# Both feed-forward products of a transformer block as seven block products each

## The chip, the cores and the metric

The kernel runs on one core of a Trainium2 chip, in one launch. The metric is the device time of a run in microseconds; the kernel before and the changed one are compared by their medians. Five engines matter here: TensorE (PE in the views; PEld is its weight load, which overlaps), VectorE (DVE), ScalarE (ACT), GpSimd (POOL) and SyncE (SP), which only issues transfers here. Each works through its own instructions in order and waits on semaphores for the others.

## The reference, cut to what matters

A block of 512 tokens with 1024 features goes through a mixing layer (attention, spatial gating, a short convolution and a pooling branch, gated and merged) and then through a feed-forward layer. Everything is float32. The change concerns the last three lines.

```python
D_MODEL = 1024; SEQ = 512; D_FF = 4 * D_MODEL; EPS = 1e-6
...
        x = x + rmsnorm(merged @ w_out[l], norm_mix_post[l])
        h = rmsnorm(x, norm_ffn_pre[l])
        f = jnp.square(jax.nn.relu(h @ w_ff1[l])) @ w_ff2[l]
        x = x + rmsnorm(f, norm_ffn_post[l])
```

## The kernel before

Matrix products keep float32 accuracy with operands in the faster format fp32r: each operand is split into a high part (a cast, on ACT) and a low part (source minus high part, on DVE), and one product of blocks is three matmuls, high by high, high by low and low by high, added up in PSUM. That is `mm3`. `load` fetches 128x1024 weights into a ring of three `raw` buffers through SP's queue, and `split_w` makes the pair `wh`, `wl` out of them, in rings of five. PE and ACT run through the wrapper `InOrder`, so all their instructions carry line 95 (in the feed-forward layer it fixes the order of PE alone); `split_w`'s subtraction is line 119.

The normalized input of the feed-forward layer is kept transposed, as `hh` and `hl` (128 partitions x 8 blocks of features x 512 tokens). `turn_h(t)` makes the part of 128 tokens: eight transposes of `yg`, the cast, the subtraction, and the sum of squares for the norm. It is called for tokens t - 1 while the output projection of the mixing layer runs for tokens t, and for the last 128 tokens in the midst of the first feed-forward blocks.

The first product has 32 blocks of 128 hidden features. Four of them (`EARLY`) start with the first 256 tokens alone, since the last 128 tokens are not ready, and get their second half afterwards; these are the only matmuls of 256 columns in this layer. Each other block is 8 x 3 matmuls of 512 columns (`ff1`). A block's result goes through relu and square on ACT into `u`, and is split by `usplit`. The second product runs in two halves of 512 output features. The first half is interleaved: after each block of the first product come 4 x 3 matmuls of 512 columns for the block ahead of it (`second`). The second half follows by itself, 32 blocks long (L805 on); its last six blocks (`LAST`) are held back, and done for 128 tokens after the other, so that norm and store of one part run beside the matmuls of the next.

SP's queue holds the transfers in program order. Each waits until the buffer that it fills is free. On ACT, DVE and POOL a scheduler sets the order by its own estimate of times; PE keeps the order of the code.

Of the kernel before, what the change touches and what calls it, by code (L numbers as in the profile page):

```python
# [80 lines left out]
def build(ctx, tc, d, out):  # L81
# [102 lines left out]
    cs = zp.tile([P, 2, NT, 16], F32, name="cs")  # L184

# [473 lines left out]
    gmix = xp.tile([P, D], F32, name="gmix")  # L659
    gffn = xp.tile([P, D], F32, name="gffn")  # L660
# [37 lines left out]
    def turn_h(t):  # L698
        for j in range(2):
# [5 lines left out]
            DVE.tensor_tensor(dst[1], pt, f(hh_)[:, 4 * j:4 * j + 4, t * P:(t + 1) * P], ALU.subtract)  # L705
        sq = wk_.tile([P, D], F32, tag="sq", name="sq", bufs=2)
# [43 lines left out]
    acc = [bank("acc") for _ in range(NT)]  # L750

    pend = []

    def usplit(j):
        uj = u[j // 8][:, j % 8, :]
        uh = us.tile([P, S], F32R, tag="uh", name="uh")
        ul = us.tile([P, S], F32R, tag="ul", name="ul")
        DVE.tensor_copy(uh, uj)
        DVE.tensor_tensor(ul, uj, f(uh), ALU.subtract)  # L759
        return uh, ul  # L760

    def ff2(dst, j, w, us_, t, first=0, last=NFF - 1):
        mm3(dst[t], sl(us_, slice(None), slice(t * P, (t + 1) * P)), sl(w, slice(None), slice((j % 2) * 512, (j % 2 + 1) * 512)),
            j == first, j == last)
# [24 lines left out]
    while pend:
        second(*pend.pop(0))  # L790
    for t in range(NT):
        sq = us.tile([P, S], F32, tag="r", name="r", bufs=2)
        ACT.activation(sq, acc[t], AF.Square, scale=r2[:, t:t + 1], accum_out=sst[:, t, 0:1])
        DVE.tensor_scalar(sst[:, t, 0:1], sst[:, t, 0:1], D * EPS, None, ALU.add)
        DVE.scalar_tensor_tensor(fo[:, t, :], acc[t], r2[:, t:t + 1], gpost[:, :512], ALU.mult, ALU.mult)
# [21 lines left out]
    for t in range(NT):
        for j, w, us_ in held:
            ff2(acc2, j, w, us_, t)
        sq = us.tile([P, S], F32, tag="r", name="r", bufs=2)  # L820
        f2 = lp.tile([P, D], F32, tag="f2", name="f2", bufs=2)
        ACT.activation(sq, acc2[t], AF.Square, scale=r2[:, t:t + 1], accum_out=sst[:, t, 1:2])
        norm_scale(sst[:, t, 2:3], sst[:, t, 3:4], sst[:, t, 0:1], sst[:, t, 1:2])
        DVE.scalar_tensor_tensor(f2[:, 512:], acc2[t], r2[:, t:t + 1], gpost[:, 512:], ALU.mult, ALU.mult)
        DVE.scalar_tensor_tensor(f2[:, :512], fo[:, t, :], sst[:, t, 2:3], x1[:, t, :512], ALU.mult, ALU.add)
        nc.sync.dma_start(out[t * P:(t + 1) * P, :512], f2[:, :512])
        DVE.scalar_tensor_tensor(f2[:, 512:], f2[:, 512:], sst[:, t, 2:3], x1[:, t, 512:], ALU.mult, ALU.add)
        nc.sync.dma_start(out[t * P:(t + 1) * P, 512:], f2[:, 512:])


def layout(i):
# [42 lines left out]
    g["w2"] = pairs(a["w_ff2"])  # L874
# [32 lines left out]
```

## Time and profile before

| | |
|---|---|
| median of 3 runs | 751.49 us (751.43 to 751.66) |
| the profiled execution | 751.82 us, of which the span from the first to the last instruction is 750.1 us |
| busy share of the span | PE 99%, PEld 84%, DVE 53%, ACT 37%, POOL 2% |
| mean granted clock of TensorE | 0.999 of full speed |
| DMA | 78.69 MB, 105 GB/s over the span |

A busy share is a mean over stages. A matmul's duration in the rows is longer than the distance to the next one's start, since matmuls are pipelined; the step from start to start is what one costs in a row of many. [...]

### The profile page before, as it was taken

How to read it: one execution, taken by the hardware profiler on the slowest of the kernel's cores; microseconds unless marked ns; L12 is line 12 of the kernel's file. 1: busy time of each engine (PE TensorE's matmuls, PEld its weight loads, DVE VectorE, ACT ScalarE, POOL GpSimd, SP SyncE). 2: the span in 40 equal slices, each digit the busy share in tenths (PEclk: the TensorE clock that was granted, in tenths of full speed). 3: DMA queues.
4: the chain of work that ended last, by engine and by line, in shares of the span. 5: the costliest groups of instructions: out<-in, count | busy, mean ns of one | idle time of the engine just before them, and what ended most of it. 6: DMA issues, size and time to landing. Idle time of an engine off the chain costs nothing.

```text
span 750.1 us, 8971 instructions
## 1 busy us (share of the span) xinstructions
PE 741.9 (99%) x3554; PEld 626.4 (84%) x3554; DVE 400.6 (53%) x673; ACT 276.3 (37%) x423; POOL 13.2 (2%) x28
## 2 busy tenths in 40 slices
PE   9999999999999999999999999999999999999996
PEld 8988888888888888888889888888888888888885
DVE  7599975366365456445376533343343343596624
ACT  6875543532332323232354422432332333321201
POOL 1110000000000000000000000000000000000001
PEclk9999999999999999999999999999999999999999
DMA  8433231272323232322304332233222223323103
GB/s 309 181 99 113 85 113 57 83 254 85 112 85 112 85 110 88 100 97 85 96 16 149 133 113 84 85 108 105 96 92 104 85 85 112 102 94 108 61 0 113
DMA packets 23146, 78.69 MB, mean 105 GB/s; under 512 B 3008, under 2 KB 3520, under 8 KB 23104
## 3 DMA queue, kind: packets, MB, share of 16 engines
q1 hardware_dynamic: 23072, 78.12, 31.2%
q8 instruction: 28, 0.46, 0.2%
q14 instruction: 14, 0.11, 0.0%
q0 software_dynamic: 32, 0.00, 0.0%
HBM read 76.01 MB, written 2.10 MB: 104 GB/s over the span
## 4 chain that ended last, share of the span: by engine, by line
PE 87%; DVE 7%; DMA 3%; ACT 2%; issue 1%; POOL 0%; SPq 0%; DVEq 0%; ACTq 0%; POOLq 0%
PE fb L95 26%; PE z L95 23%; PE acc L95 23%; PE wo L95 6%; PE y L95 6%; DMA xk<-in_x 2%; DVE wl L119 1%; DMA xT<-in_xT 1%; PE po L95 1%; DVE ql L537 1%; DVE kl L537 1%; PE s L95 0%; PE tr L95 0%; DVE m L596 0%; ACT sq L95 0%
## 5 line engine op out<-in xcount | busy, mean ns | idle before, releaser
L95 ACT CAST wh<-raw 128x1024 fp32r<-128x1024 f32 (+1 forms) x126 | 131.8, 1048 | 365.3 <-PE z L95 148.4
L119 DVE TENSOR_TENSOR wl<-raw,wh 128x1024 fp32r<-128x1024 f32 (+1 forms) x126 | 153.1, 1217 | 158.3 <-ACT wh L95 156.7
L95 PE MATMUL fb<-zh,wh 128*128 128x512 f32 x336 | 131.4, 391 | 0.1
L95 PE MATMUL fb<-zl,wh 128*128 128x512 f32 x336 | 130.9, 390 | 0.0
L95 PE MATMUL fb<-zh,wl 128*128 128x512 f32 x336 | 130.8, 389 | 0.0
L95 PE MATMUL z<-hh,wh 128*128 128x512 f32 (+1 forms) x288 | 105.4, 366 | 0.0
L95 PE MATMUL z<-hl,wh 128*128 128x512 f32 (+1 forms) x288 | 105.3, 365 | 0.0
L95 PE MATMUL z<-hh,wl 128*128 128x512 f32 (+1 forms) x288 | 105.2, 365 | 0.0
L95 PE MATMUL acc<-wh,uh 128*128 128x512 f32 x232 | 90.2, 389 | 0.0
L95 PE MATMUL acc<-wl,uh 128*128 128x512 f32 x232 | 90.2, 389 | 0.0
L95 PE MATMUL acc<-wh,ul 128*128 128x512 f32 x232 | 90.2, 389 | 0.0
L95 PEld LDWEIGHTS fb<-zh,wh 128*128 128x128 f32 x336 | 63.1, 188 | 13.3 <-DVE zc L349 0.4
L95 PEld LDWEIGHTS fb<-zh,wl 128*128 128x128 f32 x336 | 63.1, 188 | 13.2
L440 DVE TENSOR_TENSOR g<-fb,rbc 128x512 f32<-128x512 f32 x32 | 22.1, 692 | 96.8 <-PE fb L95 96.8
L95 PEld LDWEIGHTS fb<-zl,wh 128*128 128x128 f32 x336 | 63.1, 188 | 12.8
L95 PEld LDWEIGHTS z<-hh,wl 128*128 128x128 f32 x288 | 54.3, 189 | 8.8
L95 PEld LDWEIGHTS z<-hl,wh 128*128 128x128 f32 x288 | 54.3, 189 | 8.8
L95 PEld LDWEIGHTS z<-hh,wh 128*128 128x128 f32 x288 | 54.3, 189 | 8.6
L95 PEld LDWEIGHTS acc<-wl,uh 128*128 128x128 f32 x232 | 43.5, 188 | 9.1
L95 PEld LDWEIGHTS acc<-wh,uh 128*128 128x128 f32 x232 | 43.5, 188 | 9.0
L95 PEld LDWEIGHTS acc<-wh,ul 128*128 128x128 f32 x232 | 43.5, 188 | 9.0
L759 DVE TENSOR_TENSOR ul<-u,uh 128x512 fp32r<-128x512 f32 x58 | 40.1, 692 | 3.2
(253 smaller groups left out, 851.1 us busy)
## 6 DMA issues: line engine op xcount, KB each, us to landing
raw<-in_w SPq DMA_DIRECT2D x64, 512.0 KB, 3.3
raw<-in_wG SPq DMA_DIRECT2D x32, 512.0 KB, 3.4
raw<-in_wF SPq DMA_DIRECT2D x10, 512.0 KB, 3.8
raw<-in_wB SPq DMA_DIRECT2D x8, 512.0 KB, 3.3
raw<-in_wO SPq DMA_DIRECT2D x8, 512.0 KB, 3.3
xk<-in_x SPq DMA_DIRECT2D x4, 512.0 KB, 10.0
x<-in_x SPq DMA_DIRECT2D x4, 512.0 KB, 5.1
out<-f SPq DMA_DIRECT2D x8, 256.0 KB, 2.0
```

Of the source, the lines that this page charges most:

```text
L95: ins = op(*a, **k)
L119: DVE.tensor_tensor(lo[:, :n], raw[:, :n], f(hi)[:, :n], ALU.subtract)
L440: DVE.tensor_tensor(g, ps, rbc, ALU.mult)
L537: DVE.tensor_tensor(dst[1][rows, :], src, f(dst[0])[rows, :], ALU.subtract)
L759: DVE.tensor_tensor(ul, uj, f(uh), ALU.subtract)
```

## The change

Strassen's scheme (Winograd's form) multiplies 2 x 2 blocks with seven block products in place of eight, and with sums and differences of blocks ahead of them and behind.

In the first product the two halves are those of the 512 tokens (256 each), of the 1024 input features (4 blocks of 128 each), and two neighbouring blocks of 128 hidden features. Three sums of input blocks (`hsum`) are made in `turn_h` and a fourth after the early blocks (`s4`, put where `hh`'s block A21 was). The early four blocks stay as they are. Each of 14 pairs of weight blocks loads `left` and `rght`, makes four differences of 128x512 on POOL (`sub`), splits 128x1024 three times and 128x512 once, and does seven parts of 4 x 3 matmuls of 256 columns. Partial sums that are needed twice are copied out of PSUM (`small`) and added on DVE.

The second product no longer runs beside the first. It runs in three passes over 16 pairs of hidden blocks: two block products in the first, three in the second, two in the third, each product 2 x 3 matmuls of 512 columns for each pair. Weight blocks are stored as four quarters (`quads`). The differences of activations are made in place on POOL, those of weights on POOL and, one of three in the second pass, on DVE. Six pairs' quarter b21 is kept (`KEPT`); all else is loaded anew for each pass. Norm, residual and store come at the end, with the last two pairs (`LAST`) held back.

```diff
@@ turn_h @@
+        if t >= NT // 2:
+            r = slice((t - NT // 2) * P, (t - NT // 2 + 1) * P)
+            v = wk_.tile([P, 3, HK, P], F32, tag="sv", name="sv", bufs=2)
+            v1, v2, v3 = (v[:, c] for c in range(3))
+            DVE.tensor_tensor(v3, f(hh_)[:, :HK, r], pts[0], ALU.subtract)
+            POOL.tensor_tensor(v3, v3, f(hl_)[:, :HK, r], ALU.add)
+            DVE.tensor_copy(v1, pts[0])
+            DVE.tensor_tensor(v1, v1, pts[1], ALU.add)
+            DVE.tensor_tensor(v2, pts[1], v3, ALU.subtract)
+            for c in (slice(0, 1), slice(1, 3)):
+                ACT.copy(hsum[0][:, c, :, r], v[:, c])
+                DVE.tensor_tensor(hsum[1][:, c, :, r], v[:, c], f(hsum[0])[:, c, :, r], ALU.subtract)
@@ first product @@
+    POOL.tensor_tensor(s4, f(hh_)[:, HK:, :HS], f(hsum[0])[:, 1], ALU.subtract)
+    POOL.tensor_tensor(s4, s4, f(hl_)[:, HK:, :HS], ALU.add)
+    POOL.tensor_tensor(s4, s4, f(hsum[1])[:, 1], ALU.subtract)
...
+    def part(ps, w, at, a, first):
+        for k in range(HK):
+            mm3(ps[:, :HS], sl(w, slice(None), slice(at + k * P, at + (k + 1) * P)), sl(a, slice(None), k),
+                first and k == 0, k == HK - 1, not first)
+    for j in range(EARLY, NFF, 2):
+        g, h = block(j), block(j + 1)
+        left, rght = load(d["w1"][j]), load(d["w1"][j + 1])
+        w = split_w(left)
+        ta = fx.tile([P, 1024], F32, tag="T", name="T", bufs=3)
+        sub(ta[:, B1], rght[:, B1], left[:, B1])
+        sub(ta[:, B2], rght[:, B2], ta[:, B1])
+        wa = split_w(ta)
+        tb = fx.tile([P, 1024], F32, tag="T", name="T", bufs=3)
+        sub(tb[:, B1], left[:, B2], ta[:, B2])
+        sub(tb[:, B2], rght[:, B2], rght[:, B1])
+        wb = split_w(tb)
+        w22 = split_w(rght[:, B2], 512)
+        pa, pb = bank("pa"), bank("pb")
+        part(pa, w, 0, A11, True)
...
+        part(pa, wb, 512, S3, False)
+        x3 = small()
+        ACT.copy(x3, pa[:, :HS])
+        DVE.tensor_tensor(g[:, HS:], pd[:, :HS], x3, ALU.add)
+        DVE.tensor_tensor(h[:, HS:], x3, x5, ALU.add)
@@ second product, first pass @@
+        split_a(a, u[:, :, :HS])
+        POOL.tensor_tensor(u[:, 0, :HS], u[:, 0, :HS], u[:, 0, HS:], ALU.subtract)
+        POOL.tensor_tensor(u[:, 0, HS:], u[:, 0, HS:], u[:, 1, HS:], ALU.add)
+        add(pa, a, 0, w, B1, k == 0, k == HF - 1)
+        add(pb, a, 1, w, B2, k == 0, k == HF - 1)
@@ second pass @@
+        sub(rx_[:, B1], ry[:, B2], rx_[:, B1])
+        DVE.tensor_tensor(ry[:, B2], ry[:, B1], rx_[:, B1], ALU.subtract)
+        sub(rx_[:, B2], old, ry[:, B2])
+        split_a([x[:, :2] for x in a], u[:, :, HS:])
+        sub(u[:, 1, HS:], u[:, 1, HS:], u[:, 0, :HS])
+        split_a([x[:, 2] for x in a], u[:, 1, HS:])
+        w = split_w(rx_)
+        wy = split_w(ry[:, B2], 512)
+        todo = [(pc, 0, w, B1, False), (pd, 1, w, B2, False), (pa, 2, wy, B1, True)]
@@ third pass @@
+        raw, a = second_w(k, 1), acts(2)
+        sub(raw[:, B2], raw[:, B1], raw[:, B2])
+        sub(U[k][:, 1, :HS], U[k][:, 1, :HS], U[k][:, 1, HS:])
+        split_a(a, U[k][:, :, :HS])
+        w = split_w(raw)
...
+    for i in range(2):
+        rest(pa, i, 0, B2)
+        DVE.tensor_tensor(x5[i], pa[i], x5[i], ALU.add)
+        ACT.copy(c21[i], pa[i])
+        DVE.tensor_tensor(c21[i], pd[i], c21[i], ALU.add)
+        value(2 + i, 0, c21[i])
+        value(2 + i, 1, x5[i])
+        store(2 + i, (c21[i], x5[i]))
+    for i in range(2):
+        rest(pc, i, 1, B1)
+        DVE.tensor_tensor(x2[i], pc[i], x2[i], ALU.add)
+        value(i, 1, x2[i])
+        store(i, (c11[i], x2[i]))
```

How instructions stand on the engines, at three places. First DVE, where `turn_h(2)` is done and the last 128 tokens (`yg`, written last here) are made ready for their transposes; `hl` is the low part of the transposed input, `wl` that of weights. Before:

```order
L705 TENSOR_TENSOR hl<-tr_3302,hh 128x4x128
L705 TENSOR_TENSOR hl<-tr_3309,hh 128x4x128
L708 TENSOR_SCALAR stt<-stt 128x1
L690 TENSOR_SCALAR stt<-stt 128x1
L709 RECIPROCAL r_1647<-stt 128x1
L119 TENSOR_TENSOR wl<-raw,wh 128x1024
L729 SCALAR_TENSOR_TENSOR x_1644<-yg,stt,x_1644 128x512 x2
L730 TENSOR_TENSOR yg<-x_1644,gffn 128x512 x2
```

The same place with the change, from behind the second `hl` on; a `wl` and the second `yg` follow the last row:

```order
L725 TENSOR_TENSOR sv<-hh,tr_3306 128x512
L727 COPY sv<-tr_3306 128x512
L735 TENSOR_SCALAR stt<-stt 128x1
L702 TENSOR_SCALAR stt<-stt 128x1
L728 TENSOR_TENSOR sv<-sv,tr_3313 128x512
L729 TENSOR_TENSOR sv<-tr_3313,sv 128x512
L736 RECIPROCAL r_1646<-stt 128x1
L732 TENSOR_TENSOR hsl<-sv,hsh 128x4x128
L756 SCALAR_TENSOR_TENSOR x_1645<-yg,stt,x_1645 128x512
L732 TENSOR_TENSOR hsl<-sv,hsh 128x8x128
L757 TENSOR_TENSOR yg<-x_1645,gffn 128x512
L756 SCALAR_TENSOR_TENSOR x_1645<-yg,stt,x_1645 128x512
```

Five instructions of 512 elements and one of 1024 (four times 128 and eight times 128 a partition count as 512 and 1024) now stand ahead of the last `yg`; one `wl` stands ahead of it in both.

Second, POOL over the second product. Before, its last rows are these; from the output projection on it holds eight small powers for the norms and nothing else:

```order
L136 TENSOR_TENSOR rv<-rv,nhalf 128x4
L395 MEMSET zc 128x16
L421 MEMSET zc 128x2 x2
L136 TENSOR_TENSOR stt<-stt,nhalf 128x1 x4
L136 TENSOR_TENSOR sst<-sst,nhalf 128x1 x4
```

With the change, in the second pass (`raw` are weights, `u` activations; one pair is the first three rows, and the second of the two on `u` is the third pass's):

```order
L800 TENSOR_TENSOR raw_6118<-raw,raw_6118 128x512
L800 TENSOR_TENSOR raw_6118<-raw_6118,raw 128x512
L800 TENSOR_TENSOR u_3501<-u_3501 128x256 x2
L800 TENSOR_TENSOR raw_6158<-raw,raw_6158 128x512
L800 TENSOR_TENSOR raw_6158<-raw_6158,raw 128x512
```

POOL goes from 26 rows to 158 in all.

Third, DVE for one pair of the same pass (`al` is the low part of activations):

```order
L915 TENSOR_TENSOR raw<-raw,raw_6358 128x512
L875 TENSOR_TENSOR al<-u_3507,ah 128x512
L119 TENSOR_TENSOR wl<-raw_6318,wh 128x1024
L875 TENSOR_TENSOR al<-u_3507,ah 128x256
L119 TENSOR_TENSOR wl<-raw,wh 128x512
```

In the second half of the second product before, two blocks of hidden features have these:

```order
L758 CAST uh<-u_3476 128x512
L759 TENSOR_TENSOR ul<-u_3476,uh 128x512
L119 TENSOR_TENSOR wl<-raw,wh 128x1024
L758 CAST uh<-u_3476 128x512
L759 TENSOR_TENSOR ul<-u_3476,uh 128x512
```

All five with the change read two operands from SBUF and wait, directly or through a cast, for POOL's rows of the same pair or of the one ahead.

## Rows read from the trace of the kernel before

**Rows 1.** The page's head and busy times of the engines.
```profile
span 750.1 us, 8971 instructions
PE 741.9 (99%) x3554; PEld 626.4 (84%) x3554; DVE 400.6 (53%) x673; ACT 276.3 (37%) x423; POOL 13.2 (2%) x28
```
**Rows 2.** Busy time by stretch: PE, PEld, DVE, ACT, POOL, then clock, DMA share, GB/s.
```profile
8.00:10.00 2.00, 2.00 (x7) 1.90 (x7) 1.82 (x10) 0.00 (x0) 0.00 (x0) 1.00 1.01 377
500.00:550.00 50.00, 50.00 (x223) 41.38 (x222) 17.33 (x21) 16.24 (x21) 0.00 (x0) 1.00 0.30 95
```
**Rows 3.** Timeline of PE, one block of the first product: first matmul, next block's first.
```profile
463.39 0.39 PE L95 MATMUL z<-hh,wh 128*128 128x512 f32 x1
...
468.83 0.39 PE L95 MATMUL acc<-wh,uh 128*128 128x512 f32 x1
```
**Rows 4.** Timeline of PE, three early half blocks: second matmul, 72nd, transposes behind.
```profile
393.34 0.28 PE L95 MATMUL z<-hl,wh 128*128 128x256 f32 x1
...
401.74 0.28 PE L95 MATMUL z<-hh,wl 128*128 128x256 f32 x1
401.86 1.04 PE L95 MATMUL tr<-ident,yg 128*128 128x128 f32 x8
```
**Rows 5.** Timeline of DVE ahead of those transposes.
```profile
395.06 1.28 DVE L705 TENSOR_TENSOR hl<-tr,hh 128x512 fp32r<-128x512 f32 x2
...
396.52 1.21 DVE L119 TENSOR_TENSOR wl<-raw,wh 128x1024 fp32r<-128x1024 f32 x1
398.16 1.42 DVE L729 SCALAR_TENSOR_TENSOR x<-yg,stt,x 128x512 f32<-128x512 f32 x2 [0.44 <-POOL stt L136]
399.49 1.29 DVE L730 TENSOR_TENSOR yg<-x,gffn 128x512 f32<-128x512 f32 x2
```
**Rows 6.** Groups of DVE instructions: busy us, mean ns, idle time ahead.
```profile
L119 DVE TENSOR_TENSOR wl<-raw,wh 128x1024 fp32r<-128x1024 f32 x124 | 151.6, 1223 | 158.3 <-ACT wh L95 156.7 <-issue 0.3
L759 DVE TENSOR_TENSOR ul<-u,uh 128x512 fp32r<-128x512 f32 x58 | 40.1, 692 | 3.2
L634 DVE TENSOR_TENSOR al<-oT,ah 128x256 fp32r<-128x256 f32 x4 | 1.7, 418 | 0.2 <-ACT ah L95 0.2
```
**Rows 7.** Groups of ACT instructions.
```profile
L95 ACT CAST wh<-raw 128x1024 fp32r<-128x1024 f32 x124 | 130.5, 1053 | 365.3 <-PE z L95 148.4 <-issue 105.5 <-PE acc L95 61.3
L95 ACT CAST mh<-g 128x512 fp32r<-128x512 f32 x8 | 5.0, 622 | 6.1 <-DVE g L458 6.1
```
**Rows 8.** Timeline of POOL.
```profile
2.97 0.29 POOL L156 TENSOR_SCALAR_AFFINE_SELECT mask<-mask 128x128 f32<-128x128 f32 x1
26.42 1.04 POOL L136 TENSOR_TENSOR rx<-ssx,nhalf 128x4 f32<-128x4 f32 x1 [23.16 <-DVE ssx L298]
...
27.73 0.63 POOL L341 TENSOR_SCALAR_AFFINE_SELECT wsg<-c 128x512 f32<-128x512 f32 x1
...
43.31 1.91 POOL L136 TENSOR_TENSOR rv<-rv,nhalf 128x4 f32<-128x4 f32 x1 [9.77 <-DVE rv L364]
...
389.08 0.54 POOL L136 TENSOR_TENSOR stt<-stt,nhalf 128x1 f32<-128x1 f32 x1 [5.78 <-DVE stt L690]
396.60 1.52 POOL L136 TENSOR_TENSOR stt<-stt,nhalf 128x1 f32<-128x1 f32 x1 [6.99 <-DVE r L709]
```
**Rows 9.** DVE beside POOL: timeline at 43 us; tile `dg`, durations min/median/max.
```profile
43.14 1.22 DVE L119 TENSOR_TENSOR wl<-raw,wh 128x1024 fp32r<-128x1024 f32 x1
...
L302 DVE TENSOR_SCALAR dg<-ident,rx x4: 275/318/753, 27.5 to 28.6; 128x128 f32<-128x128 f32 x4
```
**Rows 10.** DMA issues: KB each, median us from issue to landing.
```profile
raw<-in_w SPq DMA_DIRECT2D x64, 512.0 KB, 3.3
```
**Rows 11.** Timeline of the end.
```profile
743.32 0.39 PE L95 MATMUL acc<-wh,lul 128*128 128x512 f32 x1
...
746.15 0.75 DVE L827 SCALAR_TENSOR_TENSOR f<-f,sst,x 128x512 f32<-128x512 f32 x1
```
**Rows 12.** Stretches of the end, columns as in rows 2.
```profile
746.00:748.00 2.00, 0.00 (x0) 0.00 (x0) 0.90 (x2) 0.00 (x0) 0.00 (x0) 0.99 0.46 169
748.00:750.10 2.10, 0.00 (x0) 0.00 (x0) 0.00 (x0) 0.00 (x0) 0.00 (x0) 0.50 0.24 89
```

More of the change, by code (lines that the diff above doesn't have):

```diff
@@ L750, in build @@
[L750 to L764, printed above, removed]
@@ L789, in build @@
[L789 to L795, printed above, removed]
+    HF = NFF // 2
+    U = [up.tile([P, 2, S], F32, name=f"u{j}") for j in range(HF)]
@@ new lines, in build @@
+    ACT.copy(A21[0], s4)
+    DVE.tensor_tensor(A21[1], s4, f(A21[0]), ALU.subtract)
+    A11, A12, A22, S4 = (sl(h2, slice(None), k, t) for k, t in
+                         ((slice(0, HK), slice(0, HS)), (slice(HK, KD), slice(0, HS)), (slice(HK, KD), slice(HS, S)),
+                          (slice(0, HK), slice(HS, S))))
+    S1, S2, S3 = (sl(hsum, slice(None), c) for c in range(3))
+    fx = hs.enter_context(tc.tile_pool(name="fx", bufs=1, reuse_waits="tile"))
+    B1, B2 = slice(0, 512), slice(512, 1024)
@@ L817, in build @@
[L817 to L828, printed above, removed]
+    us = ctx.enter_context(tc.tile_pool(name="us", bufs=1, reuse_waits="tile"))
@@ new lines, in build, with second_w @@
+    KEPT = 6
+    gpost = lp.tile([P, D], F32, name="gpost")
+    nc.sync.dma_start(gpost, d["gpost"].partition_broadcast(P))
+    sst = lp.tile([P, 64], F32, name="sst")[:, :4 * NT].rearrange("p (t c) -> p t c", c=4)
+    b21 = [us.tile([P, 512], F32, name=f"b{k}") for k in range(KEPT)]
+    turns = [0]
+    def second_w(k, half, n=1024):
+        turns[0] += 1
+        if turns[0] % 2:
+            raw = us.tile([P, 1024], F32, tag="raw2", name="raw2", bufs=3)
+            nc.sync.dma_start(raw[:, :n], d["w2"][k][:, half * 1024:half * 1024 + n])
+            return raw
+        return load(d["w2"][k][:, half * 1024:half * 1024 + n], n)
@@ new lines, in acts, with split_a, add @@
+    def acts(n):
+        return [us.tile([P, 3, HS], F32R, tag=f"a{c}", name=f"a{c}", bufs=2)[:, :n] for c in "hl"]
+    def split_a(dst, src):
+        ACT.copy(dst[0], src)
+        DVE.tensor_tensor(dst[1], src, f(dst[0]), ALU.subtract)
+    def add(ps, a, c, w, cols, first, last, more=False):
+        for i in range(2):
+            mm3(ps[i], sl(a, slice(None), c, slice(i * P, (i + 1) * P)), sl(w, slice(None), cols), first, last, more)
+    pa, pb = [bank("pa") for _ in range(2)], [bank("pb") for _ in range(2)]
@@ new lines, in build @@
+    for k in range(HF):
+        if k < HF - KEPT:
+            w = split_w(second_w(k, 0))
+        else:
+            raw, keep = second_w(k, 0, 512), b21[k - HF + KEPT]
+            nc.sync.dma_start(keep, d["w2"][k][:, 512:1024])
+            w = [wp.tile([P, 1024], F32R, tag=f"w{c}", name=f"w{c}", bufs=5) for c in "hl"]
+            for c, src in ((B1, raw[:, :512]), (B2, keep)):
+                ACT.copy(w[0][:, c], src)
+                DVE.tensor_tensor(w[1][:, c], src, f(w[0])[:, c], ALU.subtract)
+        u, a = U[k], acts(2)
+        split_a(a, u[:, :, :HS])
[3 more added lines that the diff above has]
+        add(pb, a, 1, w, B2, k == 0, k == HF - 1)
@@ new lines, in build @@
+    c11 = [lp.tile([P, 512], F32, name=f"c11{i}") for i in range(2)]
+    for i in range(2):
+        ACT.copy(c11[i], pa[i])
+        DVE.tensor_tensor(c11[i], pb[i], c11[i], ALU.add)
+    pc, pd = [bank("pc") for _ in range(2)], [bank("pd") for _ in range(2)]
+    for k in range(HF):
+        if k < HF - KEPT:
+            rx_ = second_w(k, 0)
+            old = rx_[:, B2]
+        else:
+            rx_, old = second_w(k, 0, 512), b21[k - HF + KEPT]
+        ry = second_w(k, 1)
+        u, a = U[k], acts(3)
+        sub(rx_[:, B1], ry[:, B2], rx_[:, B1])
[7 more added lines that the diff above has]
+        todo = [(pc, 0, w, B1, False), (pd, 1, w, B2, False), (pa, 2, wy, B1, True)]
+        if k == HF - 1:
+            todo = todo[2:] + todo[:2]
+        for ps, c, w_, cols, more in todo:
+            add(ps, a, c, w_, cols, k == 0 and not more, k == HF - 1, more)
@@ new lines, in build, with value @@
+    x2 = [lp.tile([P, 512], F32, name=f"x2{i}") for i in range(2)]
+    x5 = [lp.tile([P, 512], F32, name=f"x5{i}") for i in range(2)]
+    for i in range(2):
+        ACT.copy(x2[i], pa[i])
+    for i in range(2):
+        ACT.copy(x5[i], pc[i])
+    def value(t, hf, v):
+        sq = us.tile([P, 512], F32, tag="sq", name="sq", bufs=2)
+        ACT.activation(sq, v, AF.Square, scale=r2[:, t:t + 1], accum_out=sst[:, t, hf:hf + 1])
+        if hf == 0:
+            DVE.tensor_scalar(sst[:, t, 0:1], sst[:, t, 0:1], D * EPS, None, ALU.add)
+        DVE.scalar_tensor_tensor(v, v, r2[:, t:t + 1], gpost[:, hf * 512:(hf + 1) * 512], ALU.mult, ALU.mult)
```

117 lines of the change are left out of this document (68 added, 49 removed).

## The prediction

> **What bounds the kernel now.** I read the page first: PE is busy for 99% of the span, and every other engine is far below [rows 1]. A busy share by itself may hide slow matmuls, so the next view was the table by stretch: in 50 us of the feed-forward layer PE is full and makes about 223 matmuls, while DVE has 17 us of work, ACT 16, POOL none, and the DMA engines 30% [rows 2]. The timeline gives the price: 24 matmuls of 512 columns take 468.83 - 463.39 = 5.44 us, a step of 0.2267 us [rows 3]. So the layer is PE's alone, fewer columns are the only way to shorten it, and the three others have slack to sell. What the change must not do is use it up.
>
> **PE's own work.** Whether half-width matmuls cost half is seen where they occur now: from the 2nd to the 72nd of 256 columns, 401.74 - 393.34 = 8.40 us for 70 steps, 0.1200 us each [rows 4], 53% of a wide one. First product: 28 blocks x 24 = 672 steps of 0.2267 (152.3 us) become 14 x 84 = 1176 steps of 0.1200 (141.1 us): -11.2. Second: 768 steps become 672 of the same width: 96 x 0.2267 = -21.8. Together **-33.0 us**. [...] The rows are of these very shapes, so the sum goes by them.
>
> **DVE ahead of the last transposes.** `turn_h(2)` now has five more instructions of 512 elements and one of 1024 in front of the last `yg`. Behind each other two of 512 take 1.28, so a step is about 0.60, and one of 1024 about 1.13: 4.1 us. Of it 0.44 lies in a wait for POOL that DVE had anyway, and `yg` was ready at 399.49 + 1.29 = 400.78, 1.08 ahead of its transposes at 401.86 [rows 4, 5]. What is left, **+2.6**, is PE standing still; the instructions of `turn_h(3)` lie beside 11.5 us of early matmuls.
>
> **First pair.** POOL must make three sums of 1024 and four of 512 elements, in a mixed order, while PE does the early second halves (96 x 0.12 = 11.5 us), and ACT holds both casts of differences ahead of the relu of early block 2. With the prices below POOL is done some 12 us after the sums are ready, and ACT then has about 5 us of queue before the copy that part 4 waits for, of which PE's first three parts cover 4.3. I take **+4** (0 if POOL starts early, 8 if not).
>
> **Between the two products.** SP's rows put `gpost` and the first weights of the second product (a buffer where `hsum` was) behind PE's last matmul of the first. Then come the landing, 3.3 [rows 10], the cast, 1.05 [rows 7], and the subtraction, 1.22 [rows 6]: with hand-overs **+6**, where before no wait stood at all. PE's granted clock was still 0.99 up to 748 and 0.50 after it, with the last matmul ended at 743.7 [rows 11, 12]: it fell some 4 us after the work did. A wait of 6 us may thus cost the lower level for a while; I take **+2** (0 to 4).
>
> **The tail.** Now 6.4 us lie behind the last matmul (750.1 - 743.7) [rows 1, 11], with DVE's last start at 746.15. Then DVE has, from the end of the first of four groups of 6 matmuls on, 6 sums, 14 combined operations and 6 small ones: 6 x 0.60 + 14 x 0.67 + 6 x 0.13 and one wait for POOL of 0.7 = 14.5; PE ends 3 x 6 x 0.2267 = 4.1 after that point. So 10.4 of DVE, and 3.2 of store as now: 13.6, or **+7.2**.
>
> So far: -33.0 + 2.6 + 4 + 6 + 2 + 7.2 = -11.2.
>
> **POOL and DVE together.** This decides. No row before has a POOL sum of this size. The select of 128x512 took 0.63 and that of 128x128 0.29 [rows 8]: 0.86 ns an element and 0.19 for each. A sum reads two operands; read one after the other they make 1.72 ns: 1.07 us for 512 elements, 0.63 for 256. Lower bound: the price of one operand, 0.63 and 0.41. Upper: a power of one element takes 0.54, so that as a fixed part: 1.42 and 0.98. I take the middle, as the select is the nearest in size.
>
> Do both engines run at once? The power on 128x1 took 0.54 at 389.08, and 1.52 at 396.60, while DVE's `wl` ran from 396.52 to 397.73 [rows 5, 8]. The power on 128x4 took 1.04 at 26.42, and 1.91 at 43.31, beside a `wl` that ended at 44.36 [rows 8, 9]. The other way round: one of four equal DVE instructions took 753 ns, the rest some 300, when the select ran beside them [rows 8, 9]. So POOL and a DVE instruction with two operands in SBUF (or a fast single one) take turns. Of the short power 0.39 remained after `wl`'s end, so 0.15 of a POOL instruction does overlap.
>
> In the second pass a pair has 18 x 0.2267 = 4.08 us of PE. DVE has steps of 3 x 0.60 + 0.34 + 1.13 = 3.27 [rows 6], POOL 2 x 1.07 + 2 x 0.63 = 3.40, less 4 x 0.15: together 6.1, with hand-overs 6.2. Each alone would hide under PE; in turns they do not. 16 x 2.1 = **+34** (+11 by the lower price, +54 by the upper, 0 if they overlap). In the first and third pass DVE's 1.73 and POOL's 1.1 to 1.3 make 2.7 to 3.0 against 12 x 0.2267 = 2.72: **+5** for 32 pairs (0 to 16). In the first product a pair has 84 x 0.12 = 10.1 us, and DVE's 4.3 and POOL's 4.3 fit; but the ring of three `raw` makes each right block wait for the pair ahead, so a landing and three POOL sums form a loop: 3.3 + 3 x 1.07 = 6.5, and up to 10.2 if each first waits for a `wl`. **+4** (0 to 20).
>
> The copies and casts on ACT, some 7.8 us for a pair of 10.1, and the transfers, 1 MB in 4.08 us or 257 GB/s against 377 in a busy stretch [rows 2], are hidden by that slack; they cost nothing unless POOL's lateness moves them. Moved constants and padding: nothing, as no instruction goes with them.
>
> Sum: 750.1 - 11.2 + 34 + 5 + 4 = 781.9 of span. The profiled execution was 1.7 longer than its span, and 0.33 above the median of the runs: **783 us** forecast, some 4% slower.
>
> **The rivals.** [...]
>
> *Full blocking*, 804: if nothing overlaps, a pair of the second pass has DVE's durations 3 x 0.69 + 0.42 + 1.22 = 3.71 and POOL's 3.40, 7.1 in all, +49; the first pass 3.17 a pair, +7; the third 2.98, +4; and 4 in the first product. 750.1 - 11.2 + 49 + 11 + 4 + 1.4 = 804. [...] The 0.15 that overlapped speaks against it, the length of the long powers for it.
>
> *The weight loop bounds the first product*: a period of 11.6 in place of 10.1 adds 21 us and gives about 800. The 10.2 above is its door.
>
> *Half-width matmuls cost more than half*, so that the change does not even save on PE: only if the new operands step worse than the early ones; 14 x 84 x 0.01 = 12 us for each 10 ns. Nothing in the rows speaks for it.
>
> **How the numbers follow.** About 0.2% (1.5 us) is what a measurement of this kernel can tell from no change. Forecast, 755 to 795: 0.45. Full blocking or the loop, 795 to 812: 0.15; both, above: 0.06. Overlap, 732 to 750: 0.28. Cheap POOL, within 0.2%: 0.06. So faster 0.28, same 0.06, slower 0.66. The range goes from 736 to 812, which leaves out about 0.06 above and as much below; the forecast's own is 755 to 795.
>
> **What would show it.** Right: PE's idle time in the second pass, released by DVE's `wl`, with about 6 us a pair; POOL's sums of 512 with a long spread of durations; 6 us of PE idle ahead of the first pass; 13 us behind the last matmul. The step of 0.12 us in the parts. Wrong: a second pass of 65 us with PE full, and POOL's sums at one steady duration; then the time is near 740. If the first product's pairs are longer than 10.1 us, the loop is at work.

## The result, and where the time went

The changed kernel took **822.23 us** (median of 4 runs, 821.91 to 822.53) where the kernel before took 751.58 (751.43 to 752.01): a ratio of 1.0939, 95% interval 1.092 to 1.0958. It is 71 us slower, 39 more than forecast and 10 above the range. Of all runs in this document one, of e6, was slow (907.83 us at a granted clock of 0.754), and it is left out of the times.

The page's head and busy times of the changed kernel:

```profile
span 820.7 us, 10529 instructions
PE 733.3 (89%) x3962; PEld 625.3 (76%) x3962; DVE 573.4 (70%) x768; ACT 377.0 (46%) x622; POOL 277.4 (34%) x201
```

Against [rows 1] PE has 9 us less to do, as busy time counts it, and stands still for 87 us instead of 8. The stretches of the feed-forward layer, one row each for the 14 pairs, the first, second and third pass and the time behind the last matmul (columns as in [rows 2]: busy us and count of PE, PEld, DVE, ACT and POOL, then granted clock, DMA share, GB/s):

```profile
419.44:587.50 168.06, 146.13 (x1178) 143.18 (x1176) 122.50 (x110) 96.49 (x168) 102.22 (x55) 0.96 0.28 89
593.30:651.50 58.20, 50.02 (x192) 39.12 (x193) 51.23 (x44) 28.25 (x42) 48.87 (x39) 0.90 0.53 174
651.50:760.20 108.70, 79.34 (x289) 53.98 (x288) 90.79 (x82) 42.95 (x73) 87.29 (x66) 0.95 0.40 135
760.20:805.70 45.50, 44.60 (x193) 35.45 (x191) 37.73 (x35) 23.33 (x33) 14.04 (x9) 1.00 0.28 93
805.70:820.70 15.00, 0.01 (x1) 0.00 (x0) 10.82 (x21) 3.06 (x9) 2.65 (x4) 0.64 0.37 140
```

The forecast's sum, laid out by the same stretches, against what they took:

| stretch | forecast | measured |
|---|---|---|
| start of the first pair | 419.9 | 419.4 |
| 14 pairs | 141.1 + 4 + 4 = 149.1 | 168.0 (first 18.9, the other 13 149.2) |
| between the products | 6 + 2 (clock) | 5.8 |
| first pass | 43.5 + 2.5 | 58.2 |
| second pass | 65.3 + 34 = 99.3 | 108.7 |
| third pass | 43.5 + 2.5 | 45.5 |
| behind the last matmul | 13.6 | 15.0 |

Three rows hold the whole miss: the pairs (+19), the first pass (+12) and the second (+9).

**One collision.** Shortest, median and longest duration (ns) of POOL's first kind of sum, of DVE's `al` in the three passes, and of two DVE instructions of equal size in the pairs. Of those two the first has one operand in PSUM, the other both in SBUF:

```profile
L800 POOL TENSOR_TENSOR T<-raw x28: 1258/1730/2336, 414.5 to 569.8; 128x512 f32<-128x512 f32 x28
L875 DVE TENSOR_TENSOR al<-u,ah x64: 419/680/1781, 591.1 to 800.4; 128x512 fp32r<-128x512 f32 x48, 128x256 fp32r<-128x256 f32 x16
L844 DVE TENSOR_TENSOR u<-pd,x x14: 410/411/425, 441.8 to 587.9; 128x256 f32<-128x256 f32 x14
L845 DVE TENSOR_TENSOR u<-x x14: 407/418/1183, 442.1 to 588.2; 128x256 f32<-128x256 f32 x14
```

Alone, a POOL sum of 512 elements takes 1.26 to 1.30 us and one of 256 takes 0.73. Of the 48 `al` of 512, whose operands both lie in SBUF, 31 take some 0.68, as without POOL. The six of some 1.22 each run beside a sum of 256, the six of 1.74 to 1.78 beside one of 512; five lie in between. One of either kind, POOL's sum and then DVE's `al`:

```profile
616.50 1.07 POOL L896 TENSOR_TENSOR u<-u 128x256 f32<-128x256 f32 x1
616.89 1.23 DVE L875 TENSOR_TENSOR al<-u,ah 128x512 fp32r<-128x512 f32 x1
763.67 1.78 POOL L800 TENSOR_TENSOR raw<-raw 128x512 f32<-128x512 f32 x1 [2.18 <-DMA raw<-in_w]
764.23 1.78 DVE L875 TENSOR_TENSOR al<-u,ah 128x512 fp32r<-128x512 f32 x1
```

POOL is held up likewise: its sum of 512 goes from 1.26 to 1.74, or 2.3. So the instructions of both engines last longer where they meet, and a whole hold-up of DVE is all but some 0.2 us of what the sum takes alone: the sum of 256 that takes 0.73 holds DVE up by 0.54, the one of 512 that takes 1.28 by 1.10. L844, with one operand in PSUM, was not held up: six of its 14 run beside a POOL sum, at 0.411 each, while the six L845 that follow them take 1.18.

**The pairs run in a loop that PE is not in.** One period of 12.03 us, DVE first, then ACT, then the PE instruction that waited (idle time before an instruction and its releaser in brackets):

```profile
504.53 4.29 DVE L119 TENSOR_TENSOR wl<-T,wh 128x1024 fp32r<-128x1024 f32 x2 [2.80 <-ACT wh L95]
508.75 0.41 DVE L840 TENSOR_TENSOR u<-pc,x 128x256 f32<-128x256 f32 x1
509.08 3.67 DVE L119 TENSOR_TENSOR wl<-raw,wh 128x512 fp32r<-128x512 f32 x2
512.68 0.41 DVE L844 TENSOR_TENSOR u<-pd,x 128x256 f32<-128x256 f32 x1
...
516.56 4.28 DVE L119 TENSOR_TENSOR wl<-T,wh 128x1024 fp32r<-128x1024 f32 x2 [2.80 <-ACT wh L95]
```
```profile
513.12 2.19 ACT L95 ACTIVATE u<-u 128x512 f32<-128x512 f32 x4 [4.65 <-DVE u L844]
515.22 0.35 ACT L95 COPY x<-pc 128x256 f32<-128x256 f32 x1
515.47 1.05 ACT L95 CAST wh<-T 128x1024 fp32r<-128x1024 f32 x1
```
```profile
515.63 0.39 PE L95 MATMUL pc<-hh,wh 128*128 128x256 f32 x1 [1.97 <-ACT x L95]
```

DVE's four low parts take 7.96 where they would take some 4.4 alone (3 x 1.22 and 0.69, [rows 6]; the group L119 runs over two shapes, 512 and 1024, in its second row). Behind them stands the last sum of the pair ahead (L844), behind that ACT's four relus and squares, and behind those, in ACT's queue, the copy that part 5 waits for and the cast with which DVE's next round begins. From 504.53 to 513.09, the end of L844, the period is DVE's, 8.56 us, and from there to 516.56 ACT's, 3.47; PE has 9.8 us of work in it.

**The second pass** is the same price in POOL's own loop. A period of 6.8 us, POOL and then DVE:

```profile
686.94 1.48 POOL L800 TENSOR_TENSOR raw<-raw,raw 128x512 f32<-128x512 f32 x1
689.65 1.67 POOL L800 TENSOR_TENSOR raw<-raw,raw 128x512 f32<-128x512 f32 x1 [1.23 <-DVE raw L915]
691.28 2.52 POOL L800 TENSOR_TENSOR u<-u 128x256 f32<-128x256 f32 x2
693.76 1.47 POOL L800 TENSOR_TENSOR raw<-raw,raw 128x512 f32<-128x512 f32 x1
```
```profile
687.18 1.78 DVE L119 TENSOR_TENSOR wl<-raw,wh 128x512 fp32r<-128x512 f32 x1
688.89 0.68 DVE L915 TENSOR_TENSOR raw<-raw,raw 128x512 f32<-128x512 f32 x1
689.49 0.68 DVE L875 TENSOR_TENSOR al<-u,ah 128x512 fp32r<-128x512 f32 x1
690.09 2.31 DVE L119 TENSOR_TENSOR wl<-raw,wh 128x1024 fp32r<-128x1024 f32 x1
693.46 0.62 DVE L875 TENSOR_TENSOR al<-u,ah 128x256 fp32r<-128x256 f32 x1 [1.06 <-ACT ah L95]
```

POOL waits 1.23 for DVE's sum (L915), which stands behind a `wl` that POOL's own sum has stretched from 0.69 to 1.78; `wl` of 1024 takes 2.31 in place of the 1.22 of [rows 6].

### The profile page after: what moved, and what is told of

Same layout as the page of the kernel before. It is cut to its first block, busy times and chain, and to the rows that moved or that the text cites. A ratio compares the mean times of both kernels' runs of the same rounds, so it can differ in the third digit from the quotient of the medians.

```text
span 820.7 us, 10529 instructions
## 1 busy us (share of the span) xinstructions
PE 733.3 (89%) x3962; PEld 625.3 (76%) x3962; DVE 573.4 (70%) x768; ACT 377.0 (46%) x622; POOL 277.4 (34%) x201
## 4 chain that ended last, share of the span: by engine, by line
PE 50%; DVE 21%; issue 10%; POOL 9%; ACT 6%; DMA 3%; SPq 0%; DVEq 0%; POOLq 0%; ACTq 0%
PE fb L95 24%; DVE wl L119 7%; PE pa L95 7%; PE y L95 5%; PE pc L95 5%; PE wo L95 4%; POOL u L800 3%; POOL raw L800 3%; DVE al L875 3%; ACT u L95 2%; PE psA L95 2%; DMA raw<-in_w 1%; DVE raw L915 1%; DVE wl L892 1%; PE pb L95 1%
## 5 line engine op out<-in xcount | busy, mean ns | idle before, releaser
L119 DVE TENSOR_TENSOR wl<-raw,wh 128x1024 fp32r<-128x1024 f32 (+2 forms) x152 | 230.7, 1528 | 12.7 <-ACT wh L95 11.6
L95 ACT CAST wh<-raw 128x1024 fp32r<-128x1024 f32 (+2 forms) x158 | 149.3, 949 | 164.7 <-issue 105.4
L119 DVE TENSOR_TENSOR wl<-T,wh 128x1024 fp32r<-128x1024 f32 x28 | 50.3, 1812 | 44.2 <-ACT wh L95 44.2
L95 PEld LDWEIGHTS fb<-zh,wl 128*128 128x128 f32 x336 | 63.1, 188 | 13.1
L875 DVE TENSOR_TENSOR al<-u,ah 128x512 fp32r<-128x512 f32 x64 | 54.5, 854 | 24.3 <-ACT ah L95 24.0
L800 POOL TENSOR_TENSOR T<-raw 128x512 f32<-128x512 f32 x28 | 46.7, 1672 | 48.6 <-DMA raw<-in_w 48.6
L800 POOL TENSOR_TENSOR T<-raw,T 128x512 f32<-128x512 f32 x28 | 56.4, 2014 | 1.9
L95 ACT ACTIVATE u<-u 128x512 f32<-128x512 f32 x60 | 33.9, 622 | 48.2 <-DVE u L844 45.4
L95 PE MATMUL pa<-wh,ah 128*128 128x512 f32 x96 | 40.6, 423 | 17.1 <-ACT ah L95 11.2
L95 PE MATMUL pa<-wh,al 128*128 128x512 f32 x96 | 41.6, 433 | 9.4 <-DVE al L875 9.3
L800 POOL TENSOR_TENSOR raw<-raw,raw 128x512 f32<-128x512 f32 x26 | 39.4, 1517 | 10.0 <-DVE raw L915 9.8
L95 PE MATMUL pa<-wl,ah 128*128 128x512 f32 x96 | 39.2, 408 | 0.8 <-DVE wl L119 0.8
```

The source lines that it names most:

```text
L95: ins = op(*a, **k)
L119: DVE.tensor_tensor(lo[:, :n], raw[:, :n], f(hi)[:, :n], ALU.subtract)
L800: POOL.tensor_tensor(dst, a, b, ALU.subtract)
L875: DVE.tensor_tensor(dst[1], src, f(dst[0]), ALU.subtract)
```

## The experiments

Stretches in us, each from the run's own trace; "one run" had no repetition. Ratios are to the kernel before on the same chip.

| run | time, ratio (95%) | first pair | 13 pairs | gap | pass 1 | pass 2 | pass 3 | behind |
|---|---|---|---|---|---|---|---|---|
| changed | 822.23, 1.0939 (1.092 to 1.0958) | 18.9 | 149.2 | 5.8 | 58.2 | 108.7 | 45.5 | 15.0 |
| e1, sums on DVE | 763.84, 1.0164 (1.0118 to 1.0209) | 16.8 | 134.1 | 5.4 | 48.2 | 81.0 | 44.1 | 15.1 |
| e2, no sums | 739.07, one run | 9.9 | 128.8 | 5.6 | 45.9 | 67.3 | 44.1 | 15.1 |
| e3, late squares | 802.11, 1.0673 (1.0651 to 1.0696) | 18.9 | 127.6 | 6.1 | 59.3 | 108.7 | 45.2 | 15.0 |
| e4, writes only | 741.92, one run | 14.0 | 127.6 | 5.3 | 45.9 | 69.1 | 44.1 | 15.0 |
| e12, one operand | 753.44, one run | 16.2 | 127.6 | 5.4 | 47.7 | 77.0 | 44.1 | 15.0 |
| e5, all on DVE, late squares | 751.99, 1.0008 (0.9998 to 1.0017) | 9.8 | 127.6 | 6.1 | 46.1 | 81.2 | 44.1 | 15.1 |
| e8, e5 with near weights | 751.15, 0.9994 (0.9984 to 1.0003) | 9.8 | 127.6 | 5.1 | 46.6 | 81.6 | 44.1 | 15.1 |
| e10, e8 with early casts | 745.60, 0.9921 (0.9907 to 0.9934) | 9.8 | 127.6 | 1.0 | 44.4 | 82.1 | 44.1 | 15.1 |
| e7, plain second product, sums on POOL | 772.00, 1.0264 (1.024 to 1.0287) | 18.2 | 149.9 | 0 | 174.3 in all | | | 7.1 |
| e9, plain second product on e5's first | 745.19, 0.9919 (0.9904 to 0.9933) | 9.9 | 131.9 | 0 | 174.3 in all | | | 7.1 |
| e11, e9 with three casts later | 740.51, 0.9851 (0.9834 to 0.9867) | 9.8 | 127.6 | 0 | 174.3 in all | | | 7.1 |

**e1, the sums on VectorE.**

```diff
     def sub(dst, a, b):
-        POOL.tensor_tensor(dst, a, b, ALU.subtract)
+        DVE.tensor_tensor(dst, a, b, ALU.subtract)
...
-        POOL.tensor_tensor(u[:, 0, :HS], u[:, 0, :HS], u[:, 0, HS:], ALU.subtract)
-        POOL.tensor_tensor(u[:, 0, HS:], u[:, 0, HS:], u[:, 1, HS:], ALU.add)
+        DVE.tensor_tensor(u[:, 0, :HS], u[:, 0, :HS], u[:, 0, HS:], ALU.subtract)
+        DVE.tensor_tensor(u[:, 0, HS:], u[:, 0, HS:], u[:, 1, HS:], ALU.add)
```

> All sums of the pairs and of the three passes on VectorE instead of GpSimd (the three sums for the second half of the activations stay). Theory (the time goes to GpSimd's slow sums and to VectorE's reads that wait for them): pairs of the first product 10.1 to 10.5 us instead of 11.5, first pass 44 to 46 us instead of 58, second pass bound by VectorE at about 5.2 us a pair (83 us instead of 109), sum about 758 us (750 to 766). Rival (the ring of raw weights and the landings set the pace): pairs stay above 11.3 us, sum above 795. Rival (VectorE's own added work takes the gain back): sum 780 or more.

763.84, within the theory's bounds, 58 us below the changed kernel, though DVE now does POOL's work too. The pairs (10.3 us each of the 13) and the second pass (81.0) came out as foreseen; the first pass fell to 48.2, not to 44 to 46. The second pass, by stretch:

```profile
622.56:703.59 81.03, 70.07 (x289) 52.81 (x288) 81.03 (x142) 42.33 (x72) 0.00 (x0) 1.00 0.53 175
```

DVE is busy for all 81.03 us and makes 142 instructions, where it was busy for 90.79 with 82 in the changed kernel: with the sums, DVE has *less* time to spend than without them. It is now the bound at 5.06 a pair (5.2 expected).

**e2, no sums.** Edit: the calls of `sub` and the two sums of the first pass left out, factors split as loaded.

> Leaves out every GpSimd sum of the pairs and of the passes (the factors are split as loaded, same shapes). Theory: with no GpSimd work PE is full in pairs (10.1 us), first pass (44), second pass (66 to 68) and third (44); what stays is the start of the first pair in part, the gap of about 6 and the tail of 15: sum 738 to 746. Rival (order on ScalarE, rings and landings): pairs above 11 us or a second pass above 75 us, sum above 770.

739.07. Pairs, passes and gap are where the theory put them (the first pass 2 us above), so neither ring nor landing nor the order on ACT holds PE up once the sums are gone.

**e4, POOL writes and reads nothing.**

```diff
-        POOL.tensor_tensor(dst, a, b, ALU.subtract)
+        for _ in range(3 if dst.shape[-1] == 512 else 2):
+            POOL.memset(dst, 0.37)
```

> Each GpSimd sum replaced by fills of the same place that only write SBUF (three for 512 elements, two for 256), so the factors are constants there. Theory (the cost lies in both engines reading SBUF at once): VectorE's subtractions go back to 0.68 and 1.22 us beside GpSimd's work, time near that without sums, 738 to 750. Rival (any GpSimd work or its hand-overs cost it): VectorE's durations stay at 1.2 to 2.3 us, or the second pass above 90 us.

741.92. The stretches of the 13 pairs and of the second pass, and the durations of POOL's fills and DVE's `al`:

```profile
433.31:560.87 127.56, 127.56 (x1094) 127.35 (x1092) 72.75 (x103) 86.84 (x152) 74.02 (x170) 1.00 0.33 105
612.05:681.13 69.08, 66.76 (x289) 53.45 (x288) 55.49 (x81) 41.65 (x71) 53.50 (x123) 1.00 0.62 210
```
```profile
L801 POOL MEMSET raw<- x144: 518/527/536, 590.1 to 703.6; 128x512 f32 x144
L876 DVE TENSOR_TENSOR al<-u,ah x64: 417/685/693, 564.5 to 719.8; 128x512 fp32r<-128x512 f32 x48, 128x256 fp32r<-128x256 f32 x16
```

POOL is busy for 74 us of the pairs, and three fills (1.58 us) last longer than the sum that they stand for takes alone (1.26 to 1.30). Yet the longest `al` is 0.69, where it was 1.78, and PE is full. So it is not POOL's busy time, nor that others wait for its results: it is both engines reading SBUF. (A fill also waits for no operand, which shortens POOL's own chain. What the reads alone cost is seen in DVE's busy time: 55.5 us with 81 instructions in the second pass here, 90.8 with 82 in the changed kernel.)

**e12, POOL reads one operand.**

```diff
-        POOL.tensor_tensor(dst, a, b, ALU.subtract)
+        POOL.affine_select(out=dst, in_=a, compare_op=ALU.is_ge, fill=0.0, base=0,
+                           pattern=[[0, dst.shape[-1]]], channel_multiplier=1)
```

> Each GpSimd sum of the pairs and passes replaced by a select that reads one operand of the same size (a copy of it, so the factors are other numbers). Theory (each engine holds the other off while it reads, whatever the instruction): VectorE's subtraction of 512 elements grows by about 0.44 us beside a whole select of 512 (0.63 less 0.2 of fixed part) instead of 1.06 beside a sum; second pass 80 to 88 us, pairs of the first product 9.8 to 10.2, sum 757 to 768. Rival (only a second operand collides): VectorE keeps 0.68 and 1.22, second pass 66 to 70, sum 738 to 746.

753.44: 4 us below the theory's bounds, 7 above the rival's. DVE's `al` and POOL's selects of 512:

```profile
L876 DVE TENSOR_TENSOR al<-u,ah x64: 409/686/1104, 566.3 to 731.4; 128x512 fp32r<-128x512 f32 x48, 128x256 fp32r<-128x256 f32 x16
L800 POOL TENSOR_SCALAR_AFFINE_SELECT raw<-raw x42: 609/728/1588, 593.7 to 712.8; 128x512 f32<-128x512 f32 x42
```

One operand collides too. The four longest `al` grew by 0.42, as expected, each beside a select of 512; the three that grew by 0.20 meet selects of 256, which take 0.40 alone. One of each (`x2` are two selects):

```profile
601.04 1.65 POOL L800 TENSOR_SCALAR_AFFINE_SELECT u<-u 128x256 f32<-128x256 f32 x2
602.34 0.88 DVE L876 TENSOR_TENSOR al<-u,ah 128x512 fp32r<-128x512 f32 x1
688.77 0.72 POOL L800 TENSOR_SCALAR_AFFINE_SELECT raw<-raw 128x512 f32<-128x512 f32 x1 [1.82 <-DMA raw<-in_w]
688.93 1.10 DVE L876 TENSOR_TENSOR al<-u,ah 128x512 fp32r<-128x512 f32 x1
```

So in all four cases, sums and selects of 256 and 512, a whole hold-up is what POOL's instruction takes alone less some 0.2: 0.54 of 0.73, 1.10 of 1.28, 0.20 of 0.40, 0.42 of 0.61. The theory of the hold-up stands. Its forecast of the time was too high because most instructions met no select: 39 of the 48 `al` kept some 0.69, and the second pass is 77.0 instead of 80 to 88.

**e3, late squares.** POOL's sums stay; only ACT's order changes.

```diff
-        for u in (g, h):
-            ACT.activation(u, u, AF.Relu)
-            ACT.activation(u, u, AF.Square)
+        copied = ACT.copy(x3, pa[:, :HS])
+        with tc.issue_after(copied.ins):
+            square(late)
+        late = (g, h)
```

> Relu and square of a pair queued on ScalarE one pair later; GpSimd's sums stay. Theory (in the first product the collisions only cost because VectorE's stretched subtractions, then four activations, then the copy that part 5 waits for, lie in one loop of 12 us): pairs 10.1 to 10.6 us, sum 800 to 807, passes unchanged. Rival (landings of raw weights and GpSimd's sums are the loop): pairs stay at 11.5 us or more, sum 817 to 822.

802.11, 20 us below the changed kernel, with both passes as they were. Its 13 pairs:

```profile
437.60:565.20 127.60, 127.56 (x1094) 127.36 (x1092) 93.55 (x101) 84.76 (x149) 76.02 (x48) 1.00 0.33 105
```

PE is full, with all of POOL's sums beside it. So in the pairs the collisions do no harm by themselves; they did it through the four activations that stood between DVE's stretched round and the next one. (With the loop gone the engines also meet less: POOL takes 76 us for 48 sums here, some 1.58 each, against 1.84 over the 56 of the changed kernel, 103.1 us by its two groups.)

**e5, everything on VectorE, late squares.** Both edits, and the three sums into `s4` on DVE; of the change's sums only the one in `turn_h` stays on POOL.

> All sums of the feed-forward products on VectorE, those for the second half of the activations too, and relu and square one pair later. Theory (the long first pair is GpSimd's sums of 1024 colliding with the first weight sums): first pair 10 to 13 us instead of 16.8, other pairs 9.8 to 10.3, gap, passes and tail as with the sums on VectorE alone (5.4, 48, 81, 44, 15): sum 750 to 757. Rival (the first pair waits for ScalarE's queue of early activations and casts, whoever makes the sums): it stays above 15 us, sum 757 to 763.

751.99. The first pair is 9.8, better than expected. Late squares alone leave it at 18.9 (e3), so from e1's 16.8 to here it is the move of the sums of 1024. They cost something only together with the pair's other sums: e2 keeps the three on POOL without any others, and its first pair is 9.9. In e1 they hold up DVE's first two sums of weights (first row); in the changed kernel the weight sums stand between them in POOL's queue, ACT's casts wait for those, and PE for ACT (the other two rows):

```profile
410.58 5.71 DVE L800 TENSOR_TENSOR T<-raw 128x512 f32<-128x512 f32 x2
425.22 1.05 ACT L95 CAST wh<-T 128x1024 fp32r<-128x1024 f32 x1 [4.75 <-POOL T L800]
431.01 0.58 PE L95 MATMUL pa<-hsh,wh 128*128 128x256 f32 x1 [6.70 <-ACT x L95]
```

The whole first product is at PE's floor, 137.4 us. What is left above it lies in the second product.

**e8 and e10, the gap between the products.** e8 gives the first weights the ring that lies elsewhere and moves the load of `gpost` behind the first pass.

> As the run with all sums on VectorE, but the second product's first weights go to the ring that lies elsewhere than the sums of activations, and the last scale is loaded behind the first pass. Theory (the gap is a landing of 3.3 us, a cast and a subtraction behind TensorE's last part): the gap falls from 5.4 to 1.5 to 2.8 us, and the clock does not fall in the first pass: 3 to 6 us below that run. Rival (the gap is ScalarE's drain of the last pair): it stays above 4.5 us, same time within 1.5 us.

This theory fell: 5.1 us of gap instead of 6.1, 0.8 us of time. The row that now ends the wait, ACT in e8:

```profile
556.53 4.26 ACT L95 ACTIVATE u<-u 128x512 f32<-128x512 f32 x8
560.70 0.60 ACT L95 CAST ah<-u 128x512 fp32r<-128x512 f32 x1
```

Eight activations stand ahead of the first cast of activations. The landing and ACT's queue were two chains of nearly one length, and taking one away left the other. e10 takes both: three weights early, and the last two pairs' activations behind the first two casts.

```diff
+        if k == 1:
+            with tc.issue_after(cast[0]):
+                square(late)
```

> As the run with near weights, but three weights come early, and the relus and squares of the last two pairs stand behind the first two casts of activations. Theory (the gap had two chains of one length, the landing and ScalarE's queue, and taking one away left the other): gap at most 1.5 us, first pass 44 to 45 us, 4 to 6 us below that run (745 to 747). Rival (a third wait stands behind both, as the buffers lie where the sums were): gap above 3 us, time within 2 us of it.

1.0 us of gap, a first pass of 44.4 and 745.60: as expected, and 0.8% faster than the kernel before.

**e6, e7, e9, e11, the first product alone.** The second product becomes 32 plain blocks of 24 matmuls into eight banks, each weight split once, behind the first product of e5 (e6, e9, e11) or behind that of the change as it was (e7).

> The first product in seven parts as in the run before, the second as plain blocks (32 blocks of 24 matmuls into eight banks, each weight split once). Theory (seven products pay where a pair leaves VectorE slack, and not in the second product, where it saves 22 us of matmuls and costs more in start, second pass and tail): 418 us to the first pair, 140 for the pairs, some 2 of start, 174 for the second product, 7 behind it: sum 739 to 746, faster than before. Rival (the first product's 11 us are lost in its own start and pairs as well): 750 or more.

746.57 (three runs, 746.0 to 746.97), ratio 0.9932 (0.9916 to 0.9949): faster than before, just above the bound. e9 is the same kernel again.

> The same plain second product behind the first product exactly as the change has it, sums on GpSimd. Theory (the loss in the first product is its own: 168 us for the pairs where 141 would do): sum 768 to 776, 26 to 30 us above the same kernel with the sums on VectorE. Rival (the pairs were slowed by what the second product's order puts beside them): sum below 760.

772.00, with pairs of 168.1 us as in the changed kernel. The pairs' loss is their own.

> The kernel with the first product in seven parts on VectorE and a plain second product once more, for its own profile: it was 747 where its stages add up to 739. Theory (the granted clock is lower for some 10 us of full work): pairs of 9.8 us and a second product of 174 us with a few stretches at the lower clock that make 4 to 8 us together, 745 to 748. Rival (a wait that the stages of the other runs do not have): PE idle for 4 us or more in one place, clock as before.

745.19. My theory of the clock was wrong: it stood at 1.00 in the pairs and the second product, and one pair of 13.1 us had a wait, as the rival said, though of 3.0 us and not of 4:

```profile
546.50 0.39 PE L95 MATMUL pa<-hsh,wh 128*128 128x256 f32 x1 [3.00 <-ACT x L95]
```

ACT's copy stood behind a cast of the second product that waited for a buffer of the weight sums' ring.

```diff
-        ACT.copy(a[0], block(j))
+        if j < 3:
+            with tc.issue_after(second_copy.ins):
+                ACT.copy(a[0], block(j))
+        else:
+            ACT.copy(a[0], block(j))
```

> As the kernel with only the first product in seven parts, but the second product's first three casts of activations are queued behind the last pair's second copy, so that they do not take the ring of weight sums. Theory (the one pair of 13.1 us waited for a copy behind such a cast): that pair 9.9, 3 us below: 741.5 to 743. Rival (the wait moves to the start of the second product): 744 to 746.

740.51, 1 us below the bound: 1.5% faster than the kernel before, the best of all. Of the 4.7 us below e9 the edit accounts for 3.3, the one pair; 1.2 more come from the other pairs, 9.80 instead of 9.89 each, which the edit does not explain. Its pairs, second product and end:

```profile
420.81:558.20 137.39, 137.39 (x1179) 137.39 (x1178) 111.52 (x167) 95.71 (x166) 0.00 (x0) 1.00 0.34 114
558.20:732.30 174.10, 174.09 (x768) 143.77 (x766) 65.72 (x81) 54.55 (x80) 1.65 (x3) 1.00 0.26 89
732.30:739.40 7.10, 0.00 (x0) 0.00 (x0) 2.77 (x5) 0.78 (x2) 0.55 (x1) 0.74 0.39 146
```

Against e10, which differs by the second product: seven products save 96 x 0.2267 = 21.8 of matmuls, and the second pass gives back 82.1 - 65.3 = 16.8, the end 8.0, gap and first pass 1.9. That is 5 us of loss, and the medians differ by 5.1. (The two profiled executions differ by 3.7, as the pairs of e11 start 1.7 later.)

## Why the prediction was wrong

The direction was right, the size was not: 783 forecast, 822 measured, above the range's 812. The step that failed is **POOL and DVE together**, in three places, and with it the term of the first pair.

- *The price of a sum.* I took 1.07 for 512 elements and 0.63 for 256, the middle; they take 1.26 to 1.30 and 0.73.
- *Taking turns.* "0.15 of a POOL instruction does overlap" held nearly (0.2 of a sum of 256). But I counted only whether the two engines' times add up to more than PE's. In the second pass they do, and there the size was off, not the mechanism: 43.4 instead of 34. With the measured prices its own sum gives 3.27 + 4.02 - 0.60 = 6.7, with hand-overs 6.8 a pair, which is what a pair took. e4 (69.1) gives back 39.6 us of the pass, and DVE's busy time in it falls by 35.3; e1 (81.0) shows that DVE alone would do better. In the pairs they do not, and there I wrote that DVE's 4.3 and POOL's 4.3 fit in 10.1. They fit only if nothing chains them: the stretched subtractions stood in a chain with ACT's queue.
- *The loop of the first product.* I named one, a landing and three POOL sums, gave it +4 and 11.6 us as a rival's period. The 13 pairs lost 21.6 (149.2 against 127.6). The period was 11.5 on average, yet the loop was another: ACT's four activations between two rounds of DVE. e3 showed it by moving those alone. The code could have told it: a pair's relus and squares stand behind its last copy and ahead of the next pair's copies and casts, and I looked at ACT's sum (7.8 of 10.1) and not at its place.

The first pass is the same failure in a place that I had not looked at: +14.7 over PE's 43.5, where I gave it 2.5. For ten pairs it kept PE's pace (13.60 us for the five from 607.35 on). In its last six, 4.6 us each, POOL's and DVE's sums for the second pass run ahead of time between its own: the first of them on POOL starts at 623.32. With no reads on POOL the pass takes 45.9 (e4).

The other terms:

- *PE's steps.* A part's step was even less than the 0.1200 of [rows 4]: 9.80 us for 84, 0.1167, which is worth 4 us over 14 pairs.
- *DVE ahead of the transposes*, +2.6: the early second halves start 408.24 - 405.60 = 2.64 later. What I did not count is that PE's steps can be longer for a while behind this wait: the 120 early matmuls behind it took 14.09 us in e8, but 15.64 in e10, where 16 steps from 403.90 to 407.31 took 0.21 us each, and 15.74, 15.75 and 15.17 in e7, e9 and e11.
- *First pair*, +4 (0 to 8), failed: it was +9.1 over the later floor. POOL's seven sums, which by the prediction's prices add up to 10.1 (it says some 12), took 14.1, from 411.09 to 425.19, as those of 1024 took 2.39 to 3.43 each; PE stood still for 6.70 behind them, and the pair had 0.82 of the clock. e5 shows the sums to be the cause, e2 that those of 1024 do no harm by themselves.
- *Between the two products*, +6: 5.8, in part by luck, since the landing was one of two chains (e8). The clock did fall behind it, and more often than I said: the first pass had 0.90, and two pairs with a wait of 1.97 us had 0.87 and took 13.6, where others with waits of 1.5 to 2.2 kept 1.00 and took 11.6 to 12.3.
- *The tail*, 13.6: 15.0 to 15.1 in every run whose second product has seven parts.

Of the rivals, "full blocking" (804) and the weight loop had their prices met together (6.8 a pair in the second pass for 7.1, 11.5 a pair in the first product for 11.6), though neither is right as told: some 0.2 of each sum overlaps (0.73 less 0.54, 1.28 less 1.10), and the loop was another. I had given "both, above" 0.06, as if they were independent; they had one price in common, and a long one makes both likelier. That the engines overlap, to which I gave 0.28, fell: with the sums gone the time is 739.07 (e2), near the 740 that I gave it, but the sums do not hide.

## What to carry to other kernels

Before work moves to a second engine, ask what it costs the first one. Here a GpSimd sum of 256 elements held VectorE up by 0.54 us that VectorE itself does in 0.41, so that moving sums off the fuller engine made it fuller; what did not hold VectorE up here were GpSimd's fills, which only write (in e4 the longest `al` was 0.69), and a sum beside VectorE's additions with an operand in PSUM (L844, 0.411). And when slack is sold, add it up along the chain and not by engine: 8.6 us of VectorE and 3.5 of ScalarE, each below TensorE's 9.8, made a loop of 12 through the order of one queue. Where the scheme leaves such slack (the first product, once mended) it paid 1.5%; in the second product, where its sums are the bound of one pass, it gave back 26.7 us (16.8 in that pass) for 21.8 of matmuls saved.

## What was not expected of the hardware

- The hold-up follows the length of GpSimd's instruction: a subtraction of 512 elements takes 0.68 alone, 1.22 beside a sum of 256, 1.78 beside one of 512, and 0.88 or 1.10 beside a select of 256 or 512. An addition of 256 with one operand in PSUM (L844) took 0.410 to 0.425 in all 14 cases, six of them beside a sum.
- The step of a 256-column matmul was 0.1167 in most runs (9.80 a pair), but 0.1178 (9.89 or 9.90) in the pairs of e9 that had no wait, and in e2 (9.90 the first pair, 128.80 the other 13), at a granted clock of 1.00 in both. Why stays open.
